# Grouped-query attention: score slots shared by two engines, a fixed order of a unit, a warmed PE, finer first loads and stores

## Chip, cores and metric

One core of one Trainium2 chip. The metric is device time in microseconds (us), lower is better. The profiler adds its own picture of single executions: a span from the first to the last instruction, with every instruction's start and duration. The span of the profiled execution is 1.9 us shorter than its time.

Engines: PE multiplies matrices, ACT (ScalarE) computes the exponentials, DVE (VectorE) does elementwise work, POOL (GpSimd) also, SP only issues transfers. PSUM is the memory that PE writes its results to; a *slot* is a piece of it that holds one tile at a time. The *chain* is the path of work that ended last, followed back from the end of the execution: at each step to what the work had waited for. In the profile lines below, L257 is line 257 of the kernel, `pt<-sa` output and input, and x3 the number of instructions that a row merges.

## The reference

Softmax attention with 32 query heads that share 8 key/value heads, batch 8, sequence 512, head dimension 64, all float32:

```python
batch, seq, n_heads, n_kv_heads, dim = 8, 512, 32, 8, 64
scores  = np.einsum('bhqd,bhkd->bhqk', Q, K_expanded) * (1/np.sqrt(dim))
weights = np.exp(scores - scores.max(-1, keepdims=True))
weights = weights / (weights.sum(-1, keepdims=True) + 1e-10)
output  = np.einsum('bhqk,bhkd->bhqd', weights, V_expanded)
```

## The kernel before

The work is cut into 32 *units* (eight query heads of one batch). A unit has 16 *score tiles* of 128 x 1024 float32 in PSUM. For each, PE writes the tile (two matmuls) and one engine turns it into bfloat16 weights: ACT with a true exponential (12 tiles of a unit), DVE with a linear map into the bits of a bfloat16 (4 tiles). Between scores PE does *fills*: 32 output blocks (four matmuls each, weights times V) and 20 transposes that prepare Q and K of a later unit. DVE empties the output and transpose banks; POOL divides by the row sums.

PSUM holds three score slots and two slots for fills. Before, two score slots belonged to ACT and one to DVE:

```python
apsum = ctx.enter_context(tc.tile_pool(name="apsum", bufs=2, space=bass.MemoryType.PSUM))
dpsum = ctx.enter_context(tc.tile_pool(name="dpsum", bufs=1, space=bass.MemoryType.PSUM))
xpsum = ctx.enter_context(tc.tile_pool(name="xpsum", bufs=2, space=bass.MemoryType.PSUM))
# ...
    s = (dpsum if dve else apsum).tile([128, 2, S], FP32, name="sd" if dve else "sa")
```

The order of instructions is laid down when the kernel is built. A class `Plan` walks through time with fixed costs and always takes the next thing that is due: an ACT score if its slot is free now, else a DVE score, else a fill.

```python
SCORE, SCORE_LAT = 0.222, 0.436
BLOCK, TURN, X_LAT = 0.122, 0.056, 0.2
EXP, EXP_VIS = 0.904, 1.077        # ACT: pitch, and time until the slot is free
# ...
if ta <= pe + look or (first == ta and not (scoring and td <= pe)):
    kind = "act"
elif scoring and td <= pe:
    kind = "dve"
elif tf <= pe or first == tf:
    kind = "fill"
```

At the start POOL loads V first and then the Q half that the first unit needs; at the end stores are coarse:

```python
load_v(0)
load_q(0, half=1)
load_k(0)
load_q(1)
# ... in take_out(), last unit:
if u == NU - 1 and lo >= 3 * BLK:
    divide(u, lo, n, nc.vector, x[:, 0:n * D1].rearrange("p (n c) -> p n c", c=D1))
    if lo + n == UB:
        store(u, 3 * BLK, BLK, nc.sync)
    return
```

The softmax here doesn't subtract the row's maximum and nothing guards it: scores larger than these inputs give would overflow.

## Time and profile before

| | before |
|---|---|
| time, median (3 runs) | 381.35 us (380.27 to 383.28) |
| profiled execution: time, span | 384.5, 382.6 us |
| PE, ACT, DVE busy | 94%, 94%, 80% |
| first exponential starts, last one ends | 8.67, 372.30 us |

From the profile page of the kernel before, the busy time of each engine and the chain of work that ended last:

```profile
PE 359.7 (94%) x5764; PEld 226.9 (59%) x5764; DVE 305.3 (80%) x426; ACT 358.5 (94%) x387; POOL 192.3 (50%) x135
...
PE 70%; DVE 18%; DMA 3%; issue 2%; POOL 2%; ACT 1%; POOLq 0%; ACTq 0%; DVEq 0%
```

Two engines are nearly full, and the chain runs mostly through PE. The group of the exponentials on the same page (count, busy us, mean ns, idle us before them):

```profile
L257 ACT ACTIVATE pt<-sa 128x1024 bf16<-128x1024 f32 x384 | 356.0, 1058 | 8.9 <-PE sa L247 5.1
```

The same exponentials in the timeline of the first 24 us (start, us, what, in brackets the idle time before):

```profile
8.67 2.85 ACT L257 ACTIVATE pt<-sa 128x1024 bf16<-128x1024 f32 x3 [1.26 <-PE sa L247]
13.33 2.85 ACT L257 ACTIVATE pt<-sa 128x1024 bf16<-128x1024 f32 x3 [1.80 <-PE sa L247]
17.45 1.02 ACT L257 ACTIVATE pt<-sa 128x1024 bf16<-128x1024 f32 x1 [1.26 <-PE sa L247]
19.08 1.02 ACT L257 ACTIVATE pt<-sa 128x1024 bf16<-128x1024 f32 x1 [0.60 <-PE sa L247]
```

ACT stands still four times before it runs on. In a steady unit it loses time too, but the page hides it, because records of neighbouring exponentials overlap.

### The profile page before, as it was taken

What the parts mean: (1) busy time and instruction counts of PE and PEld (TensorE: products, weight loads), DVE (VectorE), ACT (ScalarE), POOL (GpSimd) and SP (SyncE); (2) the same over time, 40 slices, a digit from 0 to 9 for tenths busy, and PEclk for the clock granted to TensorE, in tenths of its full rate; (3) what the DMA queues carried; (4) which work ended last, traced back from release to release, by engine and by line L of the source; (5) the groups of instructions that cost most, each with busy time, mean ns of one, the idle gap of its engine ahead of it and who ended that gap; (6) DMA issues with size and microseconds to landing.
All of it is one profiled execution on the core that took longest, in us unless ns stands there. A gap on an engine that the chain in (4) does not pass through costs nothing.

```text
span 382.6 us, 12995 instructions
## 1 busy us (share of the span) xinstructions
PE 359.7 (94%) x5764; PEld 226.9 (59%) x5764; DVE 305.3 (80%) x426; ACT 358.5 (94%) x387; POOL 192.3 (50%) x135
## 2 busy tenths in 40 slices
PE   3799999999999999999999999999999999999990
PEld 1355566666666666566666666666666666666660
DVE  2577788888888888888887888888888888888871
ACT  3699999999999999999999999999999999999990
POOL 5225353656545475554546555355754535444452
PEclk9999999999999999999999999999999999999997
DMA  8978776596678956599765967779566996431136
GB/s 173 208 125 145 166 181 168 144 229 155 150 167 195 251 151 149 123 223 210 182 159 144 226 137 175 173 177 253 165 128 125 229 226 172 136 121 66 66 113 219
DMA packets 41961, 64.15 MB, mean 168 GB/s; under 512 B 2352, under 2 KB 33968, under 8 KB 41904
## 3 DMA queue, kind: packets, MB, share of 16 engines
q0 software_dynamic: 33776, 57.41, 66.8%
q1 hardware_dynamic: 7600, 5.64, 5.6%
q8 instruction: 45, 0.74, 0.8%
q10 hardware_dynamic: 528, 0.26, 0.2%
q14 instruction: 12, 0.10, 0.1%
HBM read 50.59 MB, written 33.55 MB: 220 GB/s over the span
## 4 chain that ended last, share of the span: by engine, by line
PE 70%; DVE 18%; DMA 3%; issue 2%; POOL 2%; ACT 1%; POOLq 0%; ACTq 0%; DVEq 0%
PE x L281 32%; PE sa L247 23%; DVE pt L265 9%; PE x L343 9%; DVE raw L301 8%; PE sd L247 6%; DMA q_nat<-in_Q_dram 3%; ACT pt L257 1%; POOL o_sb L316 1%; POOLq L480 0%; DVE inv L314 0%; POOL v_nat L229 0%; POOL out_dram L328 0%; POOL q_nat L217 0%; POOL k_nat L224 0%
## 5 line engine op out<-in xcount | busy, mean ns | idle before, releaser
L257 ACT ACTIVATE pt<-sa 128x1024 bf16<-128x1024 f32 x384 | 356.0, 1058 | 8.9 <-PE sa L247 5.1
L281 PEld LDWEIGHTS <-pt 128*128 128x128 bf16 x4096 | 149.9, 98 | 83.3 <-issue 82.1
L316 POOL TENSOR_TENSOR o_sb<-raw,inv 128x2048 f32<-128x2048 f32 (+2 forms) x33 | 115.0, 3486 | 157.0 <-DVE inv L314 157.0
L265 DVE TENSOR_SCALAR pt<-sd 128x1024 uint16<-128x1024 f32 x128 | 154.8, 1209 | 40.6 <-PE sd L247 35.1
L247 PE MATMUL sa<-qt,kt 64*128 64x512 bf16 x768 | 150.4, 390 | 0.3 <-ACT pt L257 0.3
L301 DVE COPY raw<-x 128x455 f32<-128x455 f32 (+1 forms) x161 | 92.8, 578 | 5.7 <-PE x L281 2.7
L247 PEld LDWEIGHTS <-kt 64*128 64x128 bf16 x1024 | 44.9, 94 | 31.7 <-issue 2.4
L357 DVE COPY qt<-x 128x1024 bf16<-128x1024 bf16 x63 | 43.5, 691 | 15.1 <-PE x L343 15.1
L247 PE MATMUL sd<-qt,kt 64*128 64x512 bf16 x256 | 49.9, 386 | 0.0
L343 PE MATMUL x<-ident,q_nat 128*128 128x128 bf16 x504 | 40.4, 223 | 1.9 <-DMA q_nat<-in_Q_dram 1.9
L343 PEld LDWEIGHTS <-q_nat 128*128 128x128 bf16 x504 | 28.9, 99 | 17.5 <-issue 14.2
L217 POOL DMA_DIRECT2D q_nat<-in_Q_dram x32 | 24.0, 753 | 12.6 <-PE x L343 11.9
L328 POOL DMA_DIRECT2D out_dram<-o_sb x31 | 25.2, 813 | 9.3 <-POOL o_sb L316 9.3
L281 PE MATMUL x<-v_155,pt 128*128 128x65 bf16 x512 | 23.6, 195 | 1.4 <-DVE raw L301 1.2
L281 PE MATMUL x<-v_3756,pt 128*128 128x65 bf16 x512 | 23.1, 194 | 0.7 <-DVE raw L301 0.3
L281 PE MATMUL x<-v_2773,pt 128*128 128x65 bf16 x512 | 23.1, 194 | 0.6 <-DVE raw L301 0.3
L281 PE MATMUL x<-v_1790,pt 128*128 128x65 bf16 x512 | 23.1, 194 | 0.6 <-DVE raw L301 0.5
L281 PE MATMUL x<-v_807,pt 128*128 128x65 bf16 x512 | 23.1, 194 | 0.6 <-DVE raw L301 0.3
L281 PE MATMUL x<-v_5722,pt 128*128 128x65 bf16 x512 | 23.1, 194 | 0.6 <-DVE raw L301 0.3
L281 PE MATMUL x<-v_4739,pt 128*128 128x65 bf16 x512 | 23.1, 194 | 0.6 <-DVE raw L301 0.5
L281 PE MATMUL x<-v_6705,pt 128*128 128x65 bf16 x512 | 22.3, 194 | 0.6 <-DVE raw L301 0.3
L343 PE MATMUL x<-ident,k_nat 128*128 128x128 bf16 x124 | 17.2, 224 | 0.1
(42 smaller groups left out, 74.1 us busy)
## 6 DMA issues: line engine op xcount, KB each, us to landing
out_dram<-o_sb POOLq DMA_DIRECT2D x31, 1024.0 KB, 5.6
q_nat<-in_Q_dram POOLq DMA_DIRECT2D x31, 512.0 KB, 8.1
v_nat<-in_V_dram POOLq DMA_DIRECT2D x8, 512.0 KB, 12.5
k_nat<-in_K_dram POOLq DMA_DIRECT2D x8, 512.0 KB, 10.3
kt<-kt SPq DMA_DIRECT2D x62, 64.0 KB, 2.0
out_dram<-o_sb SPq DMA_DIRECT2D x1, 512.0 KB, 5.4
out_dram<-o_sb SPq DMA_DIRECT2D x2, 256.0 KB, 5.3
q_102<-in_Q_dram ACTq DMA_DIRECT2D x1, 256.0 KB, 4.4
```

The costliest lines, as they stand in the source:

```text
L217: nc.gpsimd.dma_start(out=t[:, :, lo * D:hi * D], in_=rows(Q, b, HU * gp + lo, HU * gp + hi))
L247: nc.tensor.matmul(s[:, m, :], kt[u][64 * m:64 * m + 64, 0 if m == g else 1, kc * 128:(kc + 1) * 128], qt[u][64 * m:64 * m + 64, i, :], st ...
L257: nc.scalar.activation(out=pts[p][:, kc, :, :], in_=score.pop((p, kc)), func=mybir.ActivationFunctionType.Exp, scale=float(scale),)
L265: nc.vector.tensor_scalar(out=pts[p][:, kc, :, :].bitcast(U16), in0=score.pop((p, kc)), scalar1=float(A_schr), scalar2=float(B_schr), op0= ...
L281: nc.tensor.matmul(xs[f][:, at * D1:(at + 1) * D1], pts[u * HPG + i][:, kc, m, qc * 128:(qc + 1) * 128], v1[u // GP][:, kc, 2 * (u % GP) + ...
L301: nc.vector.tensor_copy(out=raws[u][:, lo:lo + n, :], in_=x[:, 0:n * D1])
L316: eng.tensor_tensor(out=osbs[u].rearrange("p qc h d -> p h qc d")[:, lo // SC:lo // SC + nh], in0=src[:, :, 0:D].rearrange("p (h qc) d -> ...
L328: eng.dma_start(out=rows(out, b, HU * gp + h0, HU * gp + h1), in_=osbs[u][:, :, h0:h1, :].rearrange("p qc h d -> p qc (h d)"),)
L343: nc.tensor.transpose(xs[f][:, at * 128:(at + 1) * 128], src, ident)
L357: nc.vector.tensor_copy(out=qt[u][:, 2 * part:2 * part + 2, :], in_=x)
```

## The change

Intent: any free score slot may be taken by either engine; the order of a unit becomes a fixed pattern, found ahead, with scores in batches of two or three (fewer switches between scores and fills on PE); the PE clock is brought up while the first loads fly; the first loads are ordered by need, with V's first heads as a small load of their own; weights get six buffers instead of four; the last stores are finer and stores move from POOL to SP. Cut to its core:

```diff
+    TILES = [int(c) for c in "0100010001000100"]      # which of 16 tiles DVE takes
+    SCORES = "ADAADAADAAADAAAA"                        # order of scores in a unit
+    FILL = [0, 0, 13, 0, 0, 7, 0, 0, 6, 0, 7, 0, 4, 0, 0, 15]   # fills after each score
+    ORDER = "o4 o7 K4 08 18 o7 o7 o7".split()          # order of the fills
# ... Plan: the earliest free of three slots, whoever wants it
+                        s = min(range(nslot), key=lambda i: slots[i])
-    apsum = ctx.enter_context(tc.tile_pool(name="apsum", bufs=2, ...))
-    dpsum = ctx.enter_context(tc.tile_pool(name="dpsum", bufs=1, ...))
+    spsum = ctx.enter_context(tc.tile_pool(name="spsum", bufs=1, ...))
-    pt_pool = ctx.enter_context(tc.tile_pool(name="pt", bufs=4))
+    pt_pool = ctx.enter_context(tc.tile_pool(name="pt", bufs=6))
# ... start
-        load_v(0)
-        load_q(0, half=1)
+        nc.sync.dma_start(out=v32, in_=rows(V, 0, 0, 2))
+        load_q(0, lo=HPG)
         load_k(0)
         load_q(1)
+        for _ in range(10):
+            nc.tensor.matmul(xw, warm[:, 0:128], warm, start=True, stop=True)
# ... load_v(0) follows later
# ... end
+        loose = u < 1 or u >= nu - 2     # fills may run ahead in the first and last units
-            if lo + n == UB:
-                store(u, 3 * BLK, BLK, nc.sync)
+            store(u, lo, n, nc.sync if lo + n == UB else nc.scalar)
# ... the last unit but one is divided and stored in two halves
```

As built, PE's order has 351 score batches before (223 of one tile) and 194 after (125 of three tiles).

## The prediction

> **What bounds it now.** Two engines: the page gives ACT 94%, PE 94% busy. The 384 exponentials take 1.06 us each, but start to start never less than 0.904. The Trainium skill ("ScalarE: Activation LUTs", What ACT_TABLE_LOAD costs) gives 186 ns + 0.833·N less about 93 ns of overlap, 0.946 us; the trace's 0.904 decides. A wait up to 0.15 us hides in that overlap, so the page's ACT idle time (8.9 us) understates the loss. From the timeline's starts:
> - first exponential at 8.67 us;
> - 383 x 0.904 = 346.2 us, plus 16.2 us of late starts: 4.4 in the first unit, 1.6 in the next two, about 0.35 in each of 28 steady units (period 11.19 to 11.25 against 12 x 0.904 = 10.85);
> - after the last exponential's end (372.3) 10.3 us.
>
> The steady loss is PE's: the chain of waits is 70% PE and nearly unbroken PE in a steady unit. By the timeline a score tile costs 0.22 us, an output block 0.122, a transpose 0.053, a trip from fills to scores and back 0.21. A unit has 16 tiles, 32 blocks, 20 transposes, 11 trips: 3.5 + 3.9 + 1.1 + 2.3 = 10.8 us, plus 0.4 of waits for DVE to empty output slots: 11.2.
>
> **What changes.**
> 1. The split (12 tiles ACT, 4 DVE per unit) and the arithmetic stay, so ACT's floor and DVE's load (9.5 us busy per unit) stay.
> 2. The built PE order has score batches of 3,3,3,2,2,3 per unit instead of 11 of mostly 1: five trips fewer, -1.05 us, PE about 9.7 us per unit. ACT alone bounds then. The longest fill (11 blocks, 4 transposes, 1.6 us) follows a batch of three ACT tiles, which covers it narrowly. I expect 10.87 to 10.95 us per unit: gain about 8.5 us in all, not 1.05 x 32.
> 3. Start: 10 matmuls on zeros while loads fly. The skill ("TensorE: Matmul & The Clock Gate", The HAM clock gate) says about 3.4 us of activity frees the clock; here score pairs take 0.61 us until about 19 us, then 0.39, as it says. K's first half is turned and copied alone (0.42 instead of 0.69 us). First exponential at 7.5 us (-1.2).
> 4. The first Q load no longer queues behind V on POOL; V's first heads come as a small load; six pt buffers let scores run ahead. PE stood on loads at 11.3, 13.8, 16.4 us. Of 6 us lost 2 stay: gain 4.
> 5. Tail: 12 blocks instead of 18 follow the last scores (-0.7), POOL's last divide goes to DVE and no longer holds the final one (0.8 us), stores use two queues: gain 2.5.
> 6. Stores move to SP: no gain.
>
> **Sum.** 381.35 - 8.5 - 1.2 - 4 - 2.5 = 365.2; with slip for shared slots 366.0 us, range 362.0 to 372.5. Faster by over 2% 0.92, within 2% 0.07, slower 0.01.
>
> **What would show it.** ACT start-to-start nearly all 0.904, period below 11.0; PE busy 90% or less, chain mostly ACT; first exponential below 8 us, score pairs 0.39 us from the first; about 8 us after the last exponential.
>
> **What would make it wrong.** A slot held by a late DVE tile stops ACT, which had two of its own: periods stay at 11.1 or more (+5 us). The fill after three might starve ACT. V's copy on POOL waits for its load and holds later Q loads, stalling units 1 and 2.

(The 0.946 us in it is an estimate worked out from the page's formula.)

## More of the kernel before

PE's timeline of a steady stretch:

```profile
219.49 0.39 PE L247 MATMUL sa<-qt,kt 64*128 64x512 bf16 x2
219.81 0.62 PE L343 MATMUL x<-ident,q_nat 128*128 128x128 bf16 x8
220.34 0.53 PE L281 MATMUL x<-v_3756,pt 128*128 128x65 bf16 x12
220.80 0.39 PE L247 MATMUL sa<-qt,kt 64*128 64x512 bf16 x2
```

and ACT's over the same time:

```profile
218.28 4.02 ACT L257 ACTIVATE pt<-sa 128x1024 bf16<-128x1024 f32 x4
```

Eight transposes and three blocks lie between two scores that ACT needs. Four exponentials in a row take 4.02 us here; at the pitch they have elsewhere they would take about 3.8. PE was never waiting in this stretch: it was simply doing something else when ACT ran dry.

## The result, and the profile after

The changed kernel takes 370.18 us (median of 4 runs, 369.98 to 370.31); the kernel before, with one more run on the same chip, 381.72. The ratio is 0.9696 (95% interval 0.9657 to 0.9736). Ratios are the mean time of one kernel's fast runs over that of the other's of the same rounds, so not quite the ratio of these medians. The prediction's range (362.0 to 372.5) holds the result; its middle, 366.0, is 4.2 us too low.

The page after, the same two parts:

```profile
PE 341.9 (93%) x5774; PEld 220.6 (60%) x5774; DVE 304.2 (83%) x430; ACT 355.6 (97%) x387; POOL 167.1 (45%) x105
...
PE 47%; ACT 34%; DVE 12%; DMA 2%; issue 2%; POOL 0%; ACTq 0%; DVEq 0%; POOLq 0%
```

ACT is now 97% busy and part of the chain. The start after (timeline of ACT):

```profile
7.90 1.03 ACT L265 ACTIVATE pt<-s_170 128x1024 bf16<-128x1024 f32 x1 [0.86 <-PE s_170 L254]
8.82 1.02 ACT L265 ACTIVATE pt<-s_186 128x1024 bf16<-128x1024 f32 x1
9.72 1.03 ACT L265 ACTIVATE pt<-s_196 128x1024 bf16<-128x1024 f32 x1
10.71 1.02 ACT L265 ACTIVATE pt<-s_205 128x1024 bf16<-128x1024 f32 x1
12.07 1.02 ACT L265 ACTIVATE pt<-s_217 128x1024 bf16<-128x1024 f32 x1 [0.34 <-PE s_217 L254]
```

And a steady stretch after:

```profile
208.78 1.08 ACT L265 ACTIVATE pt<-s_4554 128x1024 bf16<-128x1024 f32 x1
209.68 1.09 ACT L265 ACTIVATE pt<-s_4565 128x1024 bf16<-128x1024 f32 x1
210.59 1.10 ACT L265 ACTIVATE pt<-s_4590 128x1024 bf16<-128x1024 f32 x1
211.49 1.12 ACT L265 ACTIVATE pt<-s_4601 128x1024 bf16<-128x1024 f32 x1
212.47 1.05 ACT L265 ACTIVATE pt<-s_4631 128x1024 bf16<-128x1024 f32 x1
```

Read the ends (start plus duration), not the starts. The starts are 0.904 us apart, then once 0.98; it looks as if the last one came late. But the durations grow by 0.01 us each and then drop, so that start plus duration is 0.917 us apart throughout (209.86, 210.77, 211.69, 212.61, 213.52). By its ends, ACT never pauses here. From now on *late time* means: the distance between the ends of neighbouring exponentials minus 0.9167 us, summed. Here is the whole span of both traces:

| part of the span, us | before | after | difference | predicted |
|---|---|---|---|---|
| first exponential starts at | 8.67 | 7.90 | -0.78 | -1.2 |
| late time, first three units | 5.56 | 0.85 | -4.71 | -4 |
| late time, 28 steady units | 5.95 | 0.24 | -5.71 | -8.5 |
| late time, last unit | 0.00 | 1.10 | +1.10 | not seen |
| after the end of the last exponential | 10.34 | 5.98 | -4.35 | -2.5 |
| slip | | | | +0.8 |
| span | 382.64 | 368.19 | -14.45 | -15.4 |

The steady period, measured at ends, went from 11.21 to 11.01 us. Twelve exponentials at 0.9167 us are 11.00. The change has taken ACT to its floor.

### The profile page after: what moved, and what is told of

Read it like the earlier page. It is cut to its first block, busy times and chain, and to the rows that moved or that the text cites. A ratio compares the mean times of both kernels' runs of the same rounds, so it can differ in the third digit from the quotient of the medians.

```text
span 368.2 us, 13048 instructions
## 1 busy us (share of the span) xinstructions
PE 341.9 (93%) x5774; PEld 220.6 (60%) x5774; DVE 304.2 (83%) x430; ACT 355.6 (97%) x387; POOL 167.1 (45%) x105
## 4 chain that ended last, share of the span: by engine, by line
PE 47%; ACT 34%; DVE 12%; DMA 2%; issue 2%; POOL 0%; ACTq 0%; DVEq 0%; POOLq 0%
ACT pt L265 34%; PE x L301 27%; DVE pt L277 11%; DMA k_nat<-in_K_dram 2%; DVE raw L321 0%; PE x L362 0%; DVE o_sb L335 0%; POOL q_nat L222 0%; ACTq L265 0%; PE s_2568 L254 0%; DVEq L277 0%; DVE inv L333 0%; PE s_344 L254 0%; PE s_6778 L254 0%; PE s_6531 L254 0%
## 5 line engine op out<-in xcount | busy, mean ns | idle before, releaser
L335 POOL TENSOR_TENSOR o_sb<-raw,inv 128x2048 f32<-128x2048 f32 (+1 forms) x33 | 114.1, 3458 | 183.4 <-issue 135.8
L301 PEld LDWEIGHTS <-pt 128*128 128x128 bf16 x4096 | 134.3, 98 | 40.2 <-issue 39.4
L254 PEld LDWEIGHTS <-kt 64*128 64x128 bf16 x1024 | 51.1, 93 | 81.1 <-issue 54.8
L301 PE MATMUL x<-v_6732,pt 128*128 128x65 bf16 x512 | 18.9, 194 | 0.8 <-ACT pt L265 0.7
L301 PE MATMUL x<-v_5749,pt 128*128 128x65 bf16 x512 | 19.0, 194 | 0.0
L301 PE MATMUL x<-v_2800,pt 128*128 128x65 bf16 x512 | 19.0, 194 | 0.0
L301 PE MATMUL x<-v_3783,pt 128*128 128x65 bf16 x512 | 19.0, 194 | 0.0
L301 PE MATMUL x<-v_1817,pt 128*128 128x65 bf16 x512 | 19.0, 194 | 0.0
L301 PE MATMUL x<-v_4766,pt 128*128 128x65 bf16 x512 | 19.0, 194 | 0.0
L301 PE MATMUL x<-v_834,pt 128*128 128x65 bf16 x512 | 19.0, 194 | 0.0
L301 PE MATMUL x<-v_182,pt 128*128 128x65 bf16 x384 | 14.2, 194 | 0.0
L369 DVE COPY kt<-x 128x512 bf16<-128x512 bf16 x31 | 12.8, 414 | 0.0
L333 DVE RECIPROCAL inv<-raw 128x32 f32<-128x32 f32 (+2 forms) x34 | 11.6, 341 | 1.2
L362 PE MATMUL x<-ident,k_nat 128*128 128x128 bf16 x124 | 12.2, 219 | 0.4 <-DMA k_nat<-in_K_dram 0.4
L362 PEld LDWEIGHTS <-k_nat 128*128 128x128 bf16 x124 | 7.4, 97 | 1.0 <-DMA k_nat<-in_K_dram 0.5
L234 POOL DMA_DIRECT2D v_nat<-in_V_dram x8 | 6.1, 761 | 0.0
L229 POOL DMA_DIRECT2D k_nat<-in_K_dram x8 | 6.0, 751 | 0.0
```

Of the source, the lines that this page charges most:

```text
L234: nc.gpsimd.dma_start(out=t, in_=rows(V, b, 0, KV))
L254: nc.tensor.matmul(s[:, m, :], kt[u][64 * m:64 * m + 64, 0 if m == g else 1, kc * 128:(kc + 1) * 128], qt[u][64 * m:64 * m + 64, i, :], st ...
L301: nc.tensor.matmul(xs[f][:, at * D1:(at + 1) * D1], pts[u * HPG + i][:, kc, m, qc * 128:(qc + 1) * 128], v1[u][:, kc, 2 * i // HPG, :], st ...
L333: nc.vector.reciprocal(out=inv, in_=src[:, :, D])
L335: eng.tensor_tensor(out=osbs[u].rearrange("p qc h d -> p h qc d")[:, lo // SC:lo // SC + nh], in0=src[:, :, 0:D].rearrange("p (h qc) d -> ...
L362: nc.tensor.transpose(xs[f][:, at * 128:(at + 1) * 128], src, ident)
```

## The experiments

All are edits of the changed kernel unless said otherwise. They ran in three calls, each on another chip: eleven batches, the same batches with owned slots, the moved block and the exponential; the found order, whole stores, the tight pattern and the first order with five tiles; no warm-up, V first, stores on POOL and the second order with five tiles. Each call ran the kernel before beside them (medians 382.28, 382.18 and 381.54 us). The changed kernel was not run again in them, so differences of a few tenths of a microsecond from its 370.18 us are not safe by time alone.

### Is it the eleven trips, or the slots? Eleven batches with shared slots

```diff
-    SCORES = "ADAADAADAAADAAAA"
-    FILL = [0, 0, 13, 0, 0, 7, 0, 0, 6, 0, 7, 0, 4, 0, 0, 15]
-    ORDER = "o4 o7 K4 08 18 o7 o7 o7".split()
-    SKIP = 9
+    SCORES = "ADAAAADADAAAAAAD"
+    FILL = [7, 0, 4, 4, 7, 0, 3, 3, 0, 4, 2, 7, 0, 6, 0, 5]
+    ORDER = "o7 K4 o7 08 o7 18 o4 o7".split()
+    SKIP = 5
```

> The changed kernel with a unit order of 11 score batches (of 1 or 2 tiles) instead of 6, slots still shared freely. Trip theory (the five saved trips of 0.21 us are what took PE off the bound): PE needs about 10.8 us per unit plus some waits again, so the unit period goes from 11.00 to 11.1-11.25 us and the time to 373-377 us. Sharing theory (three slots for whoever comes next are what let ACT run on; the trips were never the limit, because 10.8 is still below ACT's 11.00): period stays at 11.00 to 11.03 and the time within 1.5 us of 370.2, though PE gets busier by some 15 us.

Measured: 371.24 us (370.65 to 372.16), correct, 347 score batches. Late time in the 27 units after the third: 0.00, period 11.00. What the two differ by is mostly the end (6.54 us after the last exponential instead of 5.98, last two units 1.30 us late instead of 1.10); the first three units lose 0.96 us instead of 0.85. PE's page line and chain in this run:

```profile
PE 357.9 (97%) x5774; PEld 220.5 (60%) x5774; DVE 306.5 (83%) x430; ACT 355.3 (96%) x387; POOL 167.2 (45%) x105
...
PE 95%; ACT 3%; DVE 1%; issue 0%; DVEq 0%; ACTq 0%
```

and its windows view over 100 steady us (the stretch, its length, then busy us of PE, PEld, DVE, ACT and POOL, each with its number of instructions; PEld is PE's loading of weights):

```profile
100.00:200.00 100.00, 100.00 (x1638) 61.90 (x1634) 86.26 (x119) 100.00 (x110) 47.64 (x28) 1.00 0.79 179
```

PE and ACT are both 100% busy, the chain is 95% PE, and yet ACT loses nothing in these units. So the trips that my prediction counted were not what had cost time, and a chain full of PE is no proof that PE is the bound. The Trainium skill ("Trainium Kernel Development and Optimization", Performance Expectations) warns that matmul busy time is a bad metric for how close a kernel is to its roofline, and this run shows the warning's use: 100% against 95% in the same stretch of the changed kernel, with the same period.

### The same batches with owned slots

```diff
-                        s = min(range(nslot), key=lambda i: slots[i])
+                        s = nslot - 1 if at_dve else min(range(nslot - 1), key=lambda i: slots[i])
```

> The changed kernel with the same batches in the same order, but slots owned again: two for ACT tiles, one for DVE tiles. Trip theory: batches alone carry the gain, so period 11.00 to 11.05 and about 370-371 us. Sharing theory: in the batches with three ACT tiles, or two around one for DVE, PE has to stand until an ACT slot comes free and the fill after it comes too late for ACT: period 11.3 us or more, 379 us or more, about as slow as before.

Measured: 403.20 us (402.95 to 403.76), ratio 1.0548 to the kernel before: the direction of the sharing theory, and far beyond its "about as slow as before". Period 12.10, ACT 1.1 us late in every unit. These batches work only with shared slots: three ACT tiles in a row have just two slots then, and from 100 to 211 us, 9.2 units, PE stood 10.2 us until ACT had emptied one (waits view: us in total, times, longest):

```profile
PE s L254 <- ACT pt L265: 10.2, 29, 0.6
```

### A found order for owned slots

The first run left a third reading: perhaps neither sharing nor batching, but an order that fits the slots. This keeps the owned slots of the run above and takes an order of 12 batches found for them:

```diff
+    SCORES = "AADAADAADAAAAADA"
+    FILL = [5, 0, 6, 3, 0, 5, 7, 0, 1, 6, 4, 3, 6, 2, 0, 4]
+    ORDER = "o7 o4 K4 o7 08 o7 18 o7".split()
+    SKIP = 3
```

> The changed kernel with slots owned again (two for ACT tiles, one for DVE tiles) and a unit order found for them: 12 score batches, nearly all of one or two tiles. Left over after the run with 11 batches are two theories of the steady gain. Sharing theory: three slots for whoever comes next are needed, so own slots cost at least the 0.2 us per unit of before: period 11.2 us or more, 376 us or more. Order theory: what the kernel before lacked was only an order that fits its slots (its own puts seven blocks between two scores that ACT needs); then own slots and even more trips than before reach ACT's floor too: period 11.00 to 11.05, 370 to 372 us, PE busy 96% or more.

(Where the text speaks of seven blocks between two scores, it misread the trace: it is the eight transposes and three blocks shown above.)

Measured: 372.54 us (372.40 to 373.13), period 11.08. The truth lies between the two theories, nearer to the order: of the 0.21 us that the kernel before lost per unit, 0.13 is won back with owned slots and even more switches (376 batches against 351), and the two orders with shared slots have the last 0.07. Whether those 0.07 need the sharing is not shown: another order for owned slots might win them too, and the old order was not run with shared slots. This run also has the six weight buffers of the change; how much of the 0.13 is order and how much is buffers was not separated.

### Is the small gap in the starts real? One block moved

```diff
-    FILL = [0, 0, 13, 0, 0, 7, 0, 0, 6, 0, 7, 0, 4, 0, 0, 15]
+    FILL = [0, 0, 13, 0, 0, 7, 0, 0, 5, 0, 8, 0, 4, 0, 0, 15]
```

> The changed kernel with one output block moved: the fill after the third batch has 5 blocks instead of 6, the next one 8 instead of 7. In the changed kernel the exponential after the six-block fill starts 0.06 to 0.09 us late by its start stamp, in every unit. Starvation theory (this late start is a real loss by PE's fill): the period falls by about 0.08 us to 10.92 and the time by 2 us to 368. Floor theory (the end-to-end pitch of the exponentials is 0.9166 us however early the next one is stamped as started; 12 x 0.9166 = 11.00 is the floor): the late start goes or moves, the end-to-end pitch and the period of 11.00 stay, the time stays within 0.5 us of 370.2.

Measured: 370.55 us (370.43 to 371.23), period 11.01. The gap at that place vanished, durations grew on to 1.17 us over 12 exponentials, then one gap of 0.11 came at another place (and two small ones of 0.01 to 0.02). Time and period stayed. The gap in the starts is bookkeeping.

### The exponential by itself

A kernel of its own, with a wrong result on purpose:

```python
for _ in range(60):                  # "alone"
    act(pt_pool.tile([128, 2, S], BF16, name="alone"))
# ... then 60 more ("beside"), with DVE reading another score tile and PE writing a third
```

> Wrong result on purpose: the exponential of the kernel measured by itself, 60 in a row on one score tile with nothing beside it, then 60 in a row with DVE reading another score tile and PE writing a third. Floor theory: end to end 0.917 us in both stretches, start to start 0.904 with the recorded duration growing by 0.012 each time until it meets some limit. Rival (contention with DVE and PE stretches 0.904 to 0.917): 0.904 end to end in the first stretch, 0.917 only in the second. By the Trainium skill's figures 0.946 in both.

Measured (212.24 us in all; one run, so its state is unknown; ACT's pitch is the only thing read from it). ACT's timeline:

```profile
2.25 55.10 ACT L52 ACTIVATE alone<-sa 128x1024 bf16<-128x1024 f32 x60 [0.24 <-PE sa L49]
56.52 55.84 ACT L52 ACTIVATE beside<-sa 128x1024 bf16<-128x1024 f32 x60
```

and the groups (busy us, mean ns of one):

```profile
L52 ACT ACTIVATE beside<-sa 128x1024 bf16<-128x1024 f32 x60 | 55.8, 2124 | 0.0
L52 ACT ACTIVATE alone<-sa 128x1024 bf16<-128x1024 f32 x60 | 55.1, 1374 | 0.2 <-PE sa L49 0.2
```

55.10 less the first duration of 1.02, over 59 steps, is 0.917 us, with nothing beside it. End to end it is 0.9167 in both stretches; start to start it is 0.904 in both. The recorded duration grows from 1.02 to 2.49 us over the 120, so the mean of the second group is 2124 ns for work that takes 917. No contention, no limit met: 0.9167 us is what this exponential costs. The skill's formula ("ScalarE: Activation LUTs", What ACT_TABLE_LOAD costs) gives an estimate of 0.946; the measurement decides.

### The start: without the warm-up, and with V first

```diff
-        for _ in range(10):
-            nc.tensor.matmul(xw, warm[:, 0:128], warm, start=True, stop=True)
+        nc.tensor.matmul(xw, warm[:, 0:128], warm, start=True, stop=True)
```

> The changed kernel with one matmul on zeros before the loads land instead of ten. If the warm clock is worth what the prediction made of it: score pairs at 0.61 us for most of the first 18 us as before, first exponential 0.3 to 0.6 us later than 7.90, late time of the first three units 1.5 to 3 us instead of 0.85, the time 371 to 373 us. If loads alone set the start: first exponential within 0.2 us, late time within 0.3 us, no change in time.

Measured: 370.70 us (370.41 to 370.79), 0.5 above the changed kernel, and 0.5 above the run with stores on POOL (below) on the same chip. First exponential at 8.08, late time of the first three units 1.74 us. Runs of the unchanged start (the changed kernel, the moved block, both runs on the end, stores on POOL) have 7.39 to 7.96 and 0.85 to 1.58. By time, on this chip, the warm-up is worth 0.5 us. In single traces, the start of the first exponential plus the late time of three units is 9.82 us here and 8.25 to 9.29 with the unchanged start. Score pairs did take 0.61 us here until about 13 us, and 0.39 from 14.2 us on (PE's timeline of this run, then that of the changed kernel, whose transposes get faster between 5.85 and 6.57 us):

```profile
8.95 0.61 PE L254 MATMUL s<-qt,kt 64*128 64x512 bf16 x2
14.22 0.39 PE L254 MATMUL s<-qt,kt 64*128 64x512 bf16 x2
```

```profile
1.18 4.45 PE L433 MATMUL x<-warm 128*128 128x512 bf16 x10 [1.18 <-DVE warm L421]
5.42 0.63 PE L445 MATMUL x<-ident,k_106 128*128 128x128 bf16 x4
6.57 0.38 PE L445 MATMUL x<-ident,k_106 128*128 128x128 bf16 x4 [0.16 <-DVE kt L446]
```

"No change in time" was as wrong as 371 to 373.

```diff
+        load_v(0)
         load_q(0, lo=HPG)
         load_k(0)
         load_q(1)
# ... and not later
-        load_v(0)
```

> The changed kernel with the whole V load of the first batch ahead of the Q, K and Q loads on POOL again, as before the change. If the order of loads is what saved the first units: the second half of the first Q lands near 11.3 us instead of 8.8, K near 13.8 instead of 11.4, PE stands there, and the late time of the first three units goes from 0.85 to 3 to 5 us, the time to 372.5-374.5 us. If room to run ahead (six buffers) is what saved them: late time below 1.5 us, time within 0.7 us of 370.2.

Measured: 372.75 us (371.91 to 372.97), late time of the first three units 4.33 us. PE and ACT in its timelines:

```profile
11.00 0.40 PE L362 MATMUL x<-ident,q_nat 128*128 128x128 bf16 x4 [2.76 <-DMA q_nat<-in_Q_dram]
```

```profile
11.76 1.94 ACT L265 ACTIVATE pt<-s 128x1024 bf16<-128x1024 f32 x2 [2.42 <-PE s L254]
```

PE can take the half of Q up at 11.00 us instead of 8.84 (the brackets give its idle time), and ACT stands for 2.42 us behind it. By time the old order costs 2.55 us against the run with stores on POOL, on the same chip. First exponential plus late time is 11.73 us here, 14.23 in the kernel before and 8.25 to 9.29 with the unchanged start: the order of four loads carries 2.4 to 3.5 us of the 5.5 that the start gained (0.78 and 4.71 in the table above), about half, with the six buffers and the warm-up in place. No run took the buffers back to four.

A part of that goes through PE's clock; how much was not separated. The trace has the clock that PE was granted, a share of full speed, third from the end in the windows view. After PE's long pause it fell to half, from 11.73 to 18.55 us:

```profile
11.80:18.50 6.70, 6.09 (x36) 2.61 (x34) 3.96 (x5) 5.67 (x6) 1.91 (x2) 0.50 1.24 206
```

It also fell, from 12.34 to 15.75 us, in the run with stores on POOL, whose start is that of the changed kernel:

```profile
12.40:15.70 3.30, 3.17 (x20) 1.38 (x17) 1.56 (x2) 2.56 (x4) 0.00 (x0) 0.50 1.24 206
```

That run and the one with the moved block, where it fell too, have the late times of 1.58 and 1.54 us; the changed kernel and both runs on the end, where it did not, have 0.85 to 0.94. So 0.85 is what a start without such a fall gives; the next execution may have one.

### The end: whole stores, and fills kept to the pattern

```diff
-            store(u, lo, n, nc.sync if lo + n == UB else nc.scalar)
+            if lo + n == UB:
+                store(u, 3 * BLK, BLK, nc.sync)
# ... the last unit but one: one piece instead of two halves
         for a, b in ((0, 2 * BLK), (2 * BLK, 3 * BLK)) if last else (
-            (0, 2 * BLK), (2 * BLK, UB)
-        ) if u == NU - 2 else ((0, UB),):
+            (0, UB),
+        ):
```

> The changed kernel with the stores of the last two units as coarse as before: the last but one unit in one store of 1 MB instead of two halves, and the last eight blocks in one store of 256 KB instead of two of 128 KB on two queues. Store theory (the tail shrank mostly because little is left to be written at the end: before, 2 MB were issued in the last 11 us): of the 4.35 us that the tail gained 2 us or more come back, about 372-373 us, with the last store landing in 4 us or more. Compute theory (the shorter chain of blocks and the divide on DVE made the gain): at most 0.7 us come back.

Measured: 371.03 us (370.37 to 371.61), the stretch after the last exponential 6.78 instead of 5.98 us. So 0.8 us of the 4.35 belong to the finer stores, a little more than the compute theory allowed and far less than the store theory asked.

```diff
-                loose = u < 1 or u >= nu - 2
+                loose = u < 1 or u >= nu
```

> The changed kernel with the last two units kept to the pattern, where it lets fills run ahead of scores there. In the changed kernel ACT loses 1.1 us in the last unit, its only late starts after the first two. If those come from fills that run ahead: late time of the last unit below 0.4 us, and since the last scores are followed by 12 blocks in both, the span shrinks by 0.7 to 1.1 us, to about 367.3 (369.2 us timed). If the late starts come from the end itself (transposes gone, output blocks bunched), they stay and so does the time.

Measured: 371.65 us (371.28 to 372.11), the opposite of what I expected. The last unit loses 3.29 us instead of 1.10 and the stretch after it shrinks only to 5.12. When the transposes run out, the pattern's fills are all output blocks, twice as long as the transposes, and the fixed counts put up to 15 of them between scores; before the scores at 361.06 us PE even stands 0.71 us for weights that ACT has yet to compute. Letting fills go by time in the last units is better than this pattern. What causes the 1.10 us is not shown, and no other order of the last units was tried.

### Stores on POOL again

```diff
-                later.append((now + wait, lambda a=a, b=b: store(u, a, b - a, nc.sync)))
+                later.append((now + wait, lambda a=a, b=b: store(u, a, b - a, nc.sync if last else nc.gpsimd)))
```

> The changed kernel with the stores of all units but the last issued by POOL again, as before. Predicted as worth nothing: POOL gets 0.8 us per unit more to do and stays near half busy, the period stays at 11.00 us and the time within 0.7 us of 370.2. If the move to SP mattered (later issue of Q loads behind stores, or buffers freed later), periods above 11.02 or stalls of single units.

Measured: 370.20 us (370.03 to 370.45), period 11.00, POOL 52% busy instead of 45%. Worth nothing, as predicted.

### If ACT is the floor, lower it: five tiles for DVE

```diff
-    TILES = [int(c) for c in "0100010001000100"]
-    SCORES = "ADAADAADAAADAAAA"
-    FILL = [0, 0, 13, 0, 0, 7, 0, 0, 6, 0, 7, 0, 4, 0, 0, 15]
-    SKIP = 9
+    TILES = [int(c) for c in "0100100100100100"]
+    SCORES = "DAAADAADAADAADAA"
+    FILL = [0, 0, 10, 0, 8, 5, 0, 0, 9, 0, 0, 9, 0, 0, 7, 4]
+    SKIP = 11
```

> The changed kernel with five of a unit's 16 tiles on DVE instead of four, in an order found for it. Floor theory: ACT's floor falls to 11 x 0.9167 = 10.08 us per unit; DVE, busy 9.5 us of a unit, gets one tile of 1.1 to 1.2 us more and becomes the bound at 10.6 to 10.8 us: gain 6 to 12 us, 358 to 364 us. If instead the order and the slots were the limit, no gain or a loss. The result may be refused for accuracy, as 31% of the exponentials instead of 25% are the coarse kind.

Measured: 358.03 us (356.92 to 360.86), correct, ratio 0.9367 to the kernel before. Period 10.61 us, ACT late by 0.5 us in each unit: it is no longer the bound. The time is just inside the range of the floor theory; that DVE is the bound then, as it says, is not shown (PE 98%, DVE 96% busy from 100 to 200 us).

Then the same split in another order:

```diff
+    TILES = [int(c) for c in "0100100100010010"]
+    SCORES = "AADAADAAADAADAAD"
+    FILL = [9, 0, 0, 13, 0, 0, 10, 5, 0, 0, 7, 0, 0, 8, 0, 0]
+    ORDER = "o4 K4 o7 o7 o7 08 18 o7".split()
+    SKIP = 3
```

> Five tiles of 16 on DVE as in the run that gave 358 us, in another order found for it: mostly batches of three, six trips per unit instead of seven, and ACT tiles first so that ACT starts earlier. With five tiles ACT is no longer the bound (ACT late by 0.5 us in every unit, PE 96% and DVE 93% busy, chain 93% PE), so now trips should count: one trip of 0.21 us less gives a period of 10.40 to 10.55 instead of 10.61 and a first exponential near 7.9 instead of 8.67: 352 to 356 us. If DVE with five tiles is already the bound, the period stays at 10.6 and only the start improves: 357 us.

Measured: 355.33 us (355.29 to 355.46), correct, ratio 0.9301 (0.9261 to 0.9342). Period 10.51, first exponential at 8.11 us. Its page:

```profile
PE 336.9 (95%) x5774; PEld 226.0 (64%) x5774; DVE 328.9 (93%) x462; ACT 335.0 (95%) x355; POOL 167.2 (47%) x105
...
DVE 63%; PE 28%; issue 5%; ACT 2%; DVEq 0%; ACTq 0%
```

Three engines are within two points of each other, and the chain is mostly DVE's. One trip fewer gave 0.10 us of period, half of its 0.21; the order was changed as a whole, so this is no clean measure of a trip. This is the fastest version. The price is coarser arithmetic: 31% instead of 25% of the weights come from the linear map. It passed the comparison with the reference; its margin was not measured.

## Why the prediction was right, and where it was not

**Right in direction and size.** "ACT alone bounds then" holds: period 11.01 against a floor of 11.00, ACT 97% busy. The gain of the start (-4.7 against -4) holds; of its named causes the order of the loads is shown for about half of the start's 5.5 us, and the six buffers were not tested. That the sum came so near is in part luck: the steady units gave 2.8 us less than forecast, the last unit lost 1.1 and the first exponential came 0.4 less early, while the end gave 1.85 and the first units 0.7 more. Stores on SP are worth nothing, as said.

**The step that failed: "383 x 0.904 = 346.2 us" and the steady gain of 8.5 us.** The prediction took the distance of start stamps for ACT's pitch. Measured alone the pitch is 0.9167 us, so the floor of a unit is 11.00 us and not 10.85, and "10.87 to 10.95 us per unit" could not be reached by any order. Of the 0.35 us "lost" per steady unit only 0.21 was there to be won. The steady units gave 5.71 us instead of 8.5.

**The mechanism named for the steady units was not the cause.** "Five trips fewer, -1.05 us" was true of PE and beside the point: with 11 batches and shared slots the period is 11.00 as well. What the kernel before lacked was an order that has the next ACT score written in time (0.13 of 0.21 us, with the buffers); the last 0.07 came only in runs with shared slots. PE looked like the bound by its busy time and its share of the chain, but the run with 11 batches has more of both and loses nothing in a steady unit.

**A slot held by DVE** did not stop ACT, nor did the fill after three: no late time in 27 of the 28 steady units; the other one lost 0.25 us once.

**The start of the first exponential**: -0.78 instead of -1.2 in this trace, and 7.39 to 7.96 us among the runs with that start. Without the warm-up it was 8.08, so the warm clock moves this point by 0.1 to 0.7 us, less than implied.

**The end**: -4.35 instead of -2.5. The finer stores account for 0.8 by experiment. The rest is read from the traces only. From the last exponential to the end of the last store's issue, 4.74 us became 2.91 (-1.83): the prediction had -1.5 for it, fewer blocks (0.7) and the divide on DVE (0.8). From there to the end, 5.60 became 3.07 (-2.53; 3.91 with whole stores): the prediction left 1.0 for it. POOL and the stores at the end of the kernel before:

```profile
367.93 3.61 POOL L316 TENSOR_TENSOR o_sb<-raw,inv 128x2048 f32<-128x2048 f32 x1 [4.50 <-DVE inv L314]
371.83 0.79 POOL L328 DMA_DIRECT2D out_dram<-o_sb  x1 [0.30 <-POOL o_sb L316]
...
374.59 2.45 SPq L328 DMA_DIRECT2D out_dram<-o_sb  x3
374.59 0.18 DVE L314 RECIPROCAL inv<-x 128x4 f32<-128x4 f32 x1 [0.82 <-POOL o_sb L316]
```

The 1 MB store of the last unit but one was issued at 371.83, half a microsecond before the last exponential ended, and another 1 MB from 374.59 on; the transfer windows show the engines of the DMA fully busy there:

```profile
374.00:378.00 4.00, 0.00 (x0) 0.00 (x0) 0.61 (x2) 0.00 (x0) 1.55 (x2) 1.00 1.00 338
```

(The last two numbers are the DMA share and GB/s.) In the last stretch after the change they were busy about half:

```profile
364.00:368.20 4.20, 0.00 (x0) 0.00 (x0) 0.13 (x1) 0.00 (x0) 0.00 (x0) 0.57 0.55 125
```

After the change the last store of the last unit but one is issued at 357.3, 4.9 us before the last exponential ends:

```profile
355.34 1.90 POOL L335 TENSOR_TENSOR o_sb<-raw,inv 128x1024 f32<-128x1024 f32 x1 [0.82 <-DVE inv L333]
358.75 1.90 POOL L335 TENSOR_TENSOR o_sb<-raw,inv 128x1024 f32<-128x1024 f32 x1 [1.50 <-issue]
```

With whole stores it was issued at 358.5, 3.2 us before, and only 0.8 us came back. So that the earlier outputs, and not the cut of the stores, emptied the queue in time is argued from these times; no run delayed the outputs alone. The prediction counted the work that follows the last scores, and too little for the bytes that wait behind it.

**The last unit** loses 1.10 us that nobody predicted: its cause is open. Fills that go by time are not at fault by themselves: the run with the tight pattern lost 3.29.

**The base.** The terms sum to -14.45 us in the traces against -15.4 predicted; that is 0.95 of the 4.2 us of miss. The rest is that I read the losses in an execution that took 384.5 us and subtracted them from the median of 381.35. All runs of the kernel before lie between 379.97 and 385.08; those of the changed kernel within 0.4 us. What varies in the kernel before was not traced, since only one profile of it exists.

## What to carry to other kernels

When an engine should run without pause, take its pitch from a row of its instructions by themselves, and from the ends; a busy share, a chain full of one engine, or the distance of start stamps may each point to the wrong limit. With few buffers between engines, an order found for exactly those buffers was worth more here than saving switches. Once one engine is at its floor, the next gain is a different split of the work, and gains are to be subtracted from the execution in which they were read. A start that leaves PE pausing may lose its clock again: compare several traces before reading tenths of a microsecond there.

## What the Trainium skill lacked or had wrong

- "ScalarE: Activation LUTs", What ACT_TABLE_LOAD costs: 186 ns + 0.833·N less about 93 ns gives 0.946 us for 1024 elements in a row; measured alone 0.9167 us, which is 0.833·N + 64 ns if the page's slope holds (one size measured).
- "Perfetto Trace Analysis", Summary: the profiler window per engine type: it says that ACT's window begins with execution and ends with the write acknowledgement. It lacks that in a row of ACTIVATEs the recorded start runs ahead: starts 0.904 us apart, ends 0.9167 apart, the duration of equal instructions growing from 1.02 to 2.49 us over 120 of them. Ends are the ones to read.
- "TensorE: Matmul & The Clock Gate", The HAM clock gate: sustained activity frees the clock after about 3.4 us, with the start of the window left to chance. In the changed kernel ten matmuls on zeros ran from 1.18 to 5.63 us without a speed-up, and the clock was full from 6.20 us on, 5.0 us after activity began (transposes of 128 columns took 0.31 us before and 0.22 after); over the eleven runs with the warm-up it was 2.8 to 5.9 us. In the kernel before, whose PE paused up to 0.9 us between its first pieces of work, it was full only at 19.62 us, 14.5 us after activity began. What the section lacks is a length for the short pauses that hold the clock back or lose it again: in the run with stores on POOL it fell at 12.34 us, and no pause of PE in the 6.8 us before was longer than 0.81 us. The page calls the ramp less than 1% of a kernel; the run without the warm-up agrees (0.5 us of 370).
- "Trainium Kernel Development and Optimization", Performance Expectations: the warning about matmul busy time holds (100% and 95% for the same period). It could add that the chain of waits misleads in the same way: 95% PE in a run where ACT was at its floor.
